# Split weight units of the input projection, stored to DRAM by the first token half and read back by the second

## The chip, the cores and the metric

One core of one Trainium2 chip runs the kernel. The metric is the device time of one execution in microseconds (us); lower is better. TensorE (PE) does the matmuls, VectorE (DVE), ScalarE (ACT) and GpSimd (POOL) work on arrays in on-chip memory, and SyncE (SP) issues the large transfers between DRAM and on-chip memory; they go out in the order of its one queue.

## The reference, cut to what matters

Two layers work on x (1024 tokens, 1024 wide). Each has a mixer and a channel part. The mixer begins with one input projection whose columns are divided among two groups of heads:

```python
proj = h @ w_in
g_q, g_k, g_v, g_o, g_a, m_q, m_kv, m_kpe = split_cols(proj, IN_SIZES)
...
o = gla_chunked(q, k, v, log_a)
o = rms_norm(o, gla_out_norm) * jax.nn.silu(g_o...)
...
mla_out = mla_attention(q_nope, q_pe, k_nope, k_pe, mv).reshape(B, S, D_MLA)
mixed = jnp.concatenate([gla_out, mla_out.astype(gla_out.dtype)], axis=-1)
return mixed @ w_out
```

The first group is a gated linear attention (q, k, v, output gate g, decay), the second a causal softmax attention with low-rank latents. Before the mixer and the channel part h is normed and modulated by a conditioning vector that comes from c @ w_ada ("ada"); the channel part is x + gate * (relu(h W1)^2 W2). Everything is float32.

## The kernel before

**Exactness.** A float32 product is made of three matmuls in a faster rounded format: both operands are split into a high part (the rounded value) and a low part (the rest), and `mm3` (L160 to L163) adds high x high, high x low and low x high. So every weight must be split in the kernel before TensorE can use it.

**Arena.** On-chip memory holds 51 slots of 128 x 1024 float32 (`Arena`, names s..., first in, first out: the slot that has been free longest is given out first). Weights pass through it in "units" of one slot each. `load` gets a slot and issues the transfer on SP's queue, `split` gets two more slots, casts the unit to its high part (L307; ScalarE, or VectorE where the unit's two letters begin with v) and subtracts it for the low part (L308; VectorE if the second letter is v, GpSimd if it is g). `get` prepares a unit and up to three after it (`LOOKAHEAD`), as long as slots are free; `drop` gives the two slots back.

**Units of the input projection.** For each layer and each half of the tokens (A: 0 to 511, B: 512 to 1023) there are 16: four L (latents and decay, 464 columns, two k-blocks each), four qk, four v and four g. Half A and half B use the same columns of w_in, and each loads and splits them for itself. In half A the v units are cast on VectorE and subtracted on GpSimd ("vg"), the others are "ag". In half B L and qk are "av", v and g "ag".

**Order.** The order in which the program is written comes from a list of steps, and the unit table follows it:

```python
"vA E X2 R LA Ha =1 TA QA X3 Hb WA gA OA LB TB QB X4 WB gB u00 P1 vB u01 a00 P1 "
```

vA, LA, QA and gA are the projections of half A and vB, LB, QB, gB those of half B (`inproj_tok` L595, and `queries_keys` for Q). WA and WB are the score matrices of the gated linear attention (`gla_scores` L896): a chain of seven levels, each with a decay on ScalarE (L955, L957), products on GpSimd (L927, L958) and VectorE (L956, L961), 128-column score matmuls on TensorE (L912) and a masked copy on VectorE (L966, L973); at its end are VectorE's L982, L988 and L990 and the transposes L998. X2, X3 and X4 load w_ada and make conditioning rows from it on VectorE (L254, L256). u00, u01 are head units of the softmax attention, a.. its blocks. xd is a buffer in DRAM to which x is moved while its slots are wanted otherwise (L1211; read back at L1235).

A list scheduler then puts the instructions of each engine in a fixed order from estimated times, so filling matmuls of a projection stand between those of a score chain. At most eight transfers of SP's queue are under way: each waits for one of eight completion semaphores, taken in turn.

## Time and profile before

| | us |
|---|---|
| median of the runs (3) | 2334.77 |
| lowest and highest | 2326.91, 2339.45 |
| profiled execution, its own time | 2329.49 |
| its span in the trace | 2327.7 |
| busy: TensorE | 2228.0 |
| busy: VectorE | 1785.4 |
| busy: ScalarE | 1137.8 |
| busy: GpSimd | 457.3 |

The span begins with the first instruction of the trace and ends with its last. Its mean granted clock of TensorE is 0.988 of full speed. Matmuls overlap in the records (a start every 0.21 to 0.23 us, a length of some 0.38 us), so "busy" counts a stretch without a gap as full; where TensorE waits, the busy time of a stretch is less than its length, and where the granted clock is under 1 the work in it took longer.

### The profile page before, as it was taken

What the parts mean: (1) busy time and instruction counts of PE and PEld (TensorE: products, weight loads), DVE (VectorE), ACT (ScalarE), POOL (GpSimd) and SP (SyncE); (2) the same over time, 40 slices, a digit from 0 to 9 for tenths busy, and PEclk for the clock granted to TensorE, in tenths of its full rate; (3) what the DMA queues carried; (4) which work ended last, traced back from release to release, by engine and by line L of the source; (5) the groups of instructions that cost most, each with busy time, mean ns of one, the idle gap of its engine ahead of it and who ended that gap; (6) DMA issues with size and microseconds to landing.
All of it is one profiled execution on the core that took longest, in us unless ns stands there. A gap on an engine that the chain in (4) does not pass through costs nothing.

```text
span 2327.7 us, 29242 instructions
## 1 busy us (share of the span) xinstructions
PE 2228.0 (96%) x11016; PEld 1851.0 (80%) x11016; DVE 1785.4 (77%) x2453; ACT 1137.8 (49%) x1764; POOL 457.3 (20%) x326
## 2 busy tenths in 40 slices
PE   7989999999999999998999999999999999999999
PEld 4778788888788877886888888887888888887887
DVE  5987769757989788889996756986665867887794
ACT  3464647535632483433535555665365228633341
POOL 2544533410030000000074345342002000000000
PEclk9999999999999999999999999999999999999999
DMA  9632210236678655765741221004354564365562
GB/s 345 202 105 81 82 30 1 82 106 221 207 220 276 192 163 200 243 229 193 241 138 34 63 61 41 10 10 125 130 160 138 184 196 145 113 231 195 166 208 82
DMA packets 236657, 340.41 MB, mean 146 GB/s; under 512 B 11078, under 2 KB 150500, under 8 KB 236516
## 3 DMA queue, kind: packets, MB, share of 16 engines
q1 hardware_dynamic: 235968, 338.08, 44.8%
q8 instruction: 86, 1.41, 0.3%
q14 instruction: 55, 0.45, 0.1%
q10 hardware_dynamic: 548, 0.48, 0.1%
HBM read 317.54 MB, written 20.97 MB: 145 GB/s over the span
## 4 chain that ended last, share of the span: by engine, by line
PE 66%; DVE 14%; DMA 7%; ACT 2%; issue 2%; POOL 1%; SPq 0%; DVEq 0%; ACTq 0%; POOLq 0%
PE ps_m L162 9%; PE ps_m L163 9%; PE ps_m L161 8%; PE ps_s L162 6%; PE ps_s L163 6%; PE ps_s L161 6%; PE ps_g L163 4%; PE ps_g L162 4%; PE ps_g L161 4%; DMA s<-in_w_mlp_down_dram 3%; PE ps_x L163 2%; PE ps_x L162 2%; DMA s<-in_w_ada_dram 2%; PE ps_x L161 2%; DMA s<-in_w_mlp_up_dram 2%
## 5 line engine op out<-in xcount | busy, mean ns | idle before, releaser
L307 ACT CAST s<-s 128x1024 fp32r<-128x1024 f32 (+2 forms) x306 | 314.8, 1035 | 474.1 <-DVE s L304 243.2
L162 PE MATMUL ps_m<-s,s 128*128 128x512 f32 (+2 forms) x1212 | 462.2, 382 | 15.4 <-DVE s L1273 15.4
L161 PE MATMUL ps_m<-s,s 128*128 128x512 f32 (+2 forms) x1212 | 460.4, 383 | 10.4 <-ACT s L1272 3.9
L163 PE MATMUL ps_m<-s,s 128*128 128x512 f32 (+2 forms) x1212 | 459.1, 379 | 1.6 <-DVE s L308 1.5
L308 POOL TENSOR_TENSOR s<-s,s 128x1024 fp32r<-128x1024 f32 (+2 forms) x90 | 229.2, 2558 | 1051.6 <-ACT s L307 696.5
L161 PE MATMUL ps_s<-s,s 128*128 128x512 f32 (+5 forms) x928 | 356.9, 388 | 9.0 <-ACT s L719 3.1
L163 PE MATMUL ps_s<-s,s 128*128 128x512 f32 (+5 forms) x928 | 354.6, 384 | 1.8 <-DVE s L308 1.3
L162 PE MATMUL ps_s<-s,s 128*128 128x512 f32 (+5 forms) x928 | 354.7, 383 | 0.0
L308 DVE TENSOR_TENSOR s<-s,s 128x1024 fp32r<-128x1024 f32 x224 | 270.0, 1217 | 55.8 <-ACT s L307 45.6
L304 DVE TENSOR_TENSOR s<-s,s 128x1024 f32<-128x1024 f32 x160 | 198.4, 1242 | 119.0 <-DMA s<-in_w_mlp_up_dram 81.7
L162 PEld LDWEIGHTS ps_m<-s,s 128*128 128x128 f32 x1212 | 230.4, 190 | 59.1 <-DVE s L1273 18.5
L161 PEld LDWEIGHTS ps_m<-s,s 128*128 128x128 f32 x1212 | 229.3, 189 | 54.9 <-ACT s L1272 6.1
L163 PEld LDWEIGHTS ps_m<-s,s 128*128 128x128 f32 x1212 | 230.0, 190 | 42.7 <-DVE s L308 2.5
L1272 ACT CAST s<-s 128x1024 fp32r<-128x1024 f32 x140 | 146.7, 1050 | 187.6 <-DVE s L1270 57.3
L161 PEld LDWEIGHTS ps_s<-s,s 128*128 128x128 f32 x928 | 174.7, 188 | 47.2 <-ACT s L719 6.1
L163 PEld LDWEIGHTS ps_s<-s,s 128*128 128x128 f32 x928 | 175.2, 189 | 37.8 <-issue 3.0
L162 PEld LDWEIGHTS ps_s<-s,s 128*128 128x128 f32 x928 | 175.4, 189 | 32.8 <-issue 1.5
L162 PE MATMUL ps_g<-s,s 128*128 128x512 f32 (+1 forms) x506 | 195.2, 387 | 0.7 <-DVE s L1273 0.7
L161 PE MATMUL ps_g<-s,s 128*128 128x512 f32 (+1 forms) x506 | 194.6, 388 | 0.0
L163 PE MATMUL ps_g<-s,s 128*128 128x512 f32 (+1 forms) x506 | 194.4, 387 | 0.1
L1273 DVE TENSOR_TENSOR s<-s,s 128x1024 fp32r<-128x1024 f32 x140 | 173.6, 1244 | 14.9 <-ACT s L1272 11.1
L162 PE MATMUL ps_x<-s,s 128*128 128x512 f32 (+3 forms) x362 | 124.2, 344 | 1.5 <-DVE s L743 1.5
(320 smaller groups left out, 3636.1 us busy)
## 6 DMA issues: line engine op xcount, KB each, us to landing
s<-in_w_mlp_up_dram SPq DMA_DIRECT2D x192, 512.0 KB, 4.8
s<-in_w_mlp_down_dram SPq DMA_DIRECT2D x192, 512.0 KB, 4.3
s<-in_w_ada_dram SPq DMA_DIRECT2D x80, 512.0 KB, 5.1
s<-in_w_in_dram SPq DMA_DIRECT2D x48, 512.0 KB, 3.8
s<-in_w_ada_dram SPq DMA_DIRECT2D x32, 256.0 KB, 4.1
xd<-s SPq DMA_DIRECT2D x16, 512.0 KB, 4.5
s<-in_w_out_dram SPq DMA_DIRECT2D x16, 512.0 KB, 4.3
s<-xd SPq DMA_DIRECT2D x16, 512.0 KB, 3.4
```

Source lines behind the costliest of these rows:

```text
L161: PE.matmul(o, lh, rh, start=start, stop=False)
L162: PE.matmul(o, lh, rl, start=False, stop=False)
L163: PE.matmul(o, ll, rh, start=False, stop=stop)
L304: V.tensor_tensor(raw[:, :n], raw[:, :n], u.second[:, :n], op=ALU.add if u.sign > 0 else ALU.subtract)
L307: (V.tensor_copy if u.eng[-2] == "v" else S.copy)(R(u.hi[:, :n]), raw[:, :n])
L308: (V if u.eng[-1] == "v" else G).tensor_tensor(R(u.lo[:, :n]), raw[:, :n], u.hi[:, :n], op=ALU.subtract)
L1272: S.copy(R(hi), t)
L1273: V.tensor_tensor(R(lo), t, hi, op=ALU.subtract)
```

## The change

After half A has used a unit, and before its slots are given back, `drop` writes its high and low part to a buffer in DRAM (two transfers on SP's queue). The unit of half B with the same columns has `first` set to that of half A: its `load` gets two slots and reads both parts back with two transfers, and its `split` does nothing. Half B no longer reads these columns of w_in. A store can go out as soon as the cast or subtraction that wrote its data is done. All lines after L282 stand up to 17 further down in the changed kernel: L292 of before is L297, L308 is L315, L912 is L929, L927 is L944, L958 is L975, L998 is L1015 and L1211 is L1228; L294 is the reload and L344 the store.

```diff
--- before.py
+++ after.py
@@ -282,12 +282,17 @@
 
     def add_unit(src, a, b, eng):
         u = Unit()
-        u.src, u.a, u.b, u.eng, u.more, u.other, u.sign = src, a, b, eng, None, None, 0
+        u.src, u.a, u.b, u.eng, u.more, u.other, u.sign, u.first, u.dram = src, a, b, eng, None, None, 0, None, None
         units.append(u)
         return u
 
     def load(u):
         n = u.a * u.b
+        if u.first is not None:
+            u.hi, u.lo = AR.alloc(), AR.alloc()
+            for i, a in enumerate((u.hi, u.lo)):
+                nc.sync.dma_start(a[:, :n], u.first.dram[i, :, 0:n])
+            return
         u.raw = AR.alloc()
         nc.sync.dma_start(u.raw[:, :n].rearrange("p (a b) -> p a b", a=u.a), u.src)
         if u.more is not None:
@@ -298,6 +303,8 @@
             nc.sync.dma_start(u.second[:, :n].rearrange("p (a b) -> p a b", a=u.a), u.other)
 
     def split(u):
+        if u.first is not None:
+            return
         n = u.a * u.b + (0 if u.more is None else u.more.shape[-1])
         raw = u.raw
         if u.other is not None:
@@ -331,6 +338,10 @@
             ustate["loaded"] += 1
 
     def drop(u):
+        if u.dram is not None:
+            n = u.a * u.b
+            for i, a in enumerate((u.hi, u.lo)):
+                nc.sync.dma_start(u.dram[i, :, 0:n], a[:, :n])
         AR.free(u.hi, u.lo)
 
     def uw(u, j, c0, n):
@@ -368,6 +379,12 @@
             elif kind == "D":
                 d = int(rest)
                 U[l, "wo", d] = add_unit(wo[:, :, d * P:(d + 1) * P], 8, P, "ag")
+
+        for kind in ("L", "qk", "v", "g"):
+            for q in range(4):
+                one, two = U[l, 0, kind, q], U[l, 1, kind, q]
+                one.dram = dp.tile([2, P, 1024], F32, tag=f"w{kind}{q}", name=f"w{kind}{q}")
+                two.first = one
         wu = w_mlp_up[l].rearrange("(k p) n -> p k n", p=P)
         wd = w_mlp_down[l].rearrange("(k p) n -> p k n", p=P)
         for stage, order, block in (
```

How it moves the instructions is seen on three engines. The first piece is SP's queue in layer 0, half A, from the load of unit qk0 (the first 128x8x128 row) to that of unit L3 (128x2x464). Before:

```order
L292 DMA s_106_741<-in_w_in_dram 128x8x128
L245 DMA s_95_634<-in_w_ada_dram 128x1024
L245 DMA s_96_637<-in_w_ada_dram 128x1024
L292 DMA s_109_771<-in_w_in_dram 128x8x128
L292 DMA s_103_711<-in_w_in_dram 128x2x464
L1211 DMA xd<-s_9_132 128x1024
```

and with the change (wL... is the DRAM buffer of an L unit):

```order
L297 DMA s_106_783<-in_w_in_dram 128x8x128
L245 DMA s_95_674<-in_w_ada_dram 128x1024
L344 DMA wL_121<-s_67_418 128x928
L245 DMA s_96_677<-in_w_ada_dram 128x1024
L344 DMA wL_122<-s_70_424 128x928
L297 DMA s_109_815<-in_w_in_dram 128x8x128
L344 DMA wL_123<-s_83_546 128x928
L297 DMA s_103_751<-in_w_in_dram 128x2x464
L344 DMA wL_123<-s_84_547 128x928
```

Stores of L units now stand between the loads of w_ada and w_in. From the first of the four loads of x (at 35.63 us in the timeline of before) up to L3 there were 15 transfers ahead of it and are now 28, of which 13 are stores. Up to the load of X3 with which VectorE begins there were 38 and are now 66.

The second piece is GpSimd in layer 0 during WB: L958 and L927 (L975 and L944 with the change) are the products of the scores, 128x1024 subtractions those of v units of half B, and 128x640 ones those of head units. Before:

```order
L308 TENSOR_TENSOR s_261_2463<-s_259_2460,s_260_2462 128x1024
L958 TENSOR_TENSOR s_228_2020<-s_204_1846,s_232_2027 128x128x4
L927 TENSOR_TENSOR s_232_2027<-s_203_1845,s_232_2027 128x512
L958 TENSOR_TENSOR s_229_2021<-s_204_1846,s_233_2028 128x64x8
L958 TENSOR_TENSOR s_228_2020<-s_204_1846,s_232_2027 128x32x16
L958 TENSOR_TENSOR s_229_2021<-s_204_1846,s_233_2028 128x16x32
L927 TENSOR_TENSOR s_233_2028<-s_203_1845,s_233_2028 128x512
L927 TENSOR_TENSOR s_232_2027<-s_203_1845,s_232_2027 128x512
L958 TENSOR_TENSOR s_228_2020<-s_204_1846,s_232_2027 128x8x64
L308 TENSOR_TENSOR s_275_2568<-s_273_2564,s_274_2567 128x640
L308 TENSOR_TENSOR s_247_2273<-s_245_2270,s_246_2272 128x1024
L308 TENSOR_TENSOR s_250_2303<-s_248_2300,s_249_2302 128x1024
```

With the change:

```order
L975 TENSOR_TENSOR s_218_2063<-s_197_1896,s_222_2070 128x256x2
L944 TENSOR_TENSOR s_222_2070<-s_196_1895,s_222_2070 128x512
L975 TENSOR_TENSOR s_217_2062<-s_197_1896,s_221_2069 128x128x4
L944 TENSOR_TENSOR s_221_2069<-s_196_1895,s_221_2069 128x512
L975 TENSOR_TENSOR s_218_2063<-s_197_1896,s_222_2070 128x64x8
L944 TENSOR_TENSOR s_222_2070<-s_196_1895,s_222_2070 128x512
L975 TENSOR_TENSOR s_217_2062<-s_197_1896,s_221_2069 128x32x16
L944 TENSOR_TENSOR s_221_2069<-s_196_1895,s_221_2069 128x512
L975 TENSOR_TENSOR s_218_2063<-s_197_1896,s_222_2070 128x16x32
L315 TENSOR_TENSOR s_253_2538<-s_251_2534,s_252_2537 128x640
L975 TENSOR_TENSOR s_217_2062<-s_197_1896,s_221_2069 128x8x64
```

The subtractions of v units are gone, one of a head unit stands ahead of the last product.

The third piece is TensorE at the end of WA in layer 0, where the first unit of LB begins (the four 128x464 matmuls L161; s47_171 before and s4_170 with the change is its high part). Before:

```order
L912 MATMUL ps_g_1297<-s19_159_1151,s47_156_1148 128x128 x4
L912 MATMUL ps_g_1303<-s19_159_1151,s47_156_1148 128x128 x4
L998 MATMUL ps_g_1319<-cs_81,s27_128_952 128x128 x4
L998 MATMUL ps_g_1325<-cs_81,s27_128_952 128x128 x4
L161 MATMUL ps_m_1625<-s47_171_1369,s0_115_835 128x464
L161 MATMUL ps_s_1626<-s47_171_1369,s0_115_835 128x464
L161 MATMUL ps_m_1627<-s47_171_1369,s0_115_835 128x464
L161 MATMUL ps_s_1628<-s47_171_1369,s0_115_835 128x464
L1042 MATMUL ps_g_1487<-s44_80_428,s11_154_1146 128x128 x4
L1048 MATMUL ps_g_1492<-s44_80_428,s33_164_1318 128x256 x2
L162 MATMUL ps_m_1625<-s24_172_1370,s0_115_835 128x464
```

With the change:

```order
L929 MATMUL ps_g_1239<-s19_159_1207,s47_156_1204 128x128 x4
L929 MATMUL ps_g_1253<-s18_158_1206,s24_157_1205 128x128 x4
L161 MATMUL ps_m_1683<-s4_170_1425,s0_115_883 128x464
L929 MATMUL ps_g_1259<-s18_158_1206,s24_157_1205 128x128 x4
L161 MATMUL ps_s_1684<-s4_170_1425,s0_115_883 128x464
L929 MATMUL ps_g_1273<-s19_159_1207,s47_156_1204 128x128 x4
L161 MATMUL ps_m_1685<-s4_170_1425,s0_115_883 128x464
L929 MATMUL ps_g_1279<-s19_159_1207,s47_156_1204 128x128 x4
L929 MATMUL ps_g_1293<-s18_158_1206,s24_157_1205 128x128 x4
L161 MATMUL ps_s_1686<-s4_170_1425,s0_115_883 128x464
L929 MATMUL ps_g_1299<-s18_158_1206,s24_157_1205 128x128 x4
L929 MATMUL ps_g_1313<-s19_159_1207,s47_156_1204 128x128 x4
```

The four matmuls that need only the high part stand between the score matmuls now. Ahead of the first score of WA stand 78 matmuls of gA, and 62 before. Elsewhere, in the attention blocks and the channel part, TensorE's order is the same in both kernels.

## Rows read from the trace of the kernel before

**Rows 1.** Page, parts 1 and 2: busy us; GB/s in 40 slices.
```profile
PE 2228.0 (96%) x11016; PEld 1851.0 (80%) x11016; DVE 1785.4 (77%) x2453; ACT 1137.8 (49%) x1764; POOL 457.3 (20%) x326
...
GB/s 345 202 105 81 82 30 1 82 106 221 207 220 276 192 163 200 243 229 193 241 138 34 63 61 41 10 10 125 130 160 138 184 196 145 113 231 195 166 208 82
```

**Rows 2.** Page, part 5: xcount | busy, mean ns | idle before.
```profile
L307 ACT CAST s<-s 128x1024 fp32r<-128x1024 f32 (+2 forms) x306 | 314.8, 1035 | 474.1 <-DVE s L304 243.2
...
L308 POOL TENSOR_TENSOR s<-s,s 128x1024 fp32r<-128x1024 f32 (+2 forms) x90 | 229.2, 2558 | 1051.6 <-ACT s L307 696.5
...
L308 DVE TENSOR_TENSOR s<-s,s 128x1024 fp32r<-128x1024 f32 x224 | 270.0, 1217 | 55.8 <-ACT s L307 45.6
```

**Rows 3.** Page, part 6: xcount, KB each, median us to landing.
```profile
xd<-s SPq DMA_DIRECT2D x16, 512.0 KB, 4.5
...
s<-xd SPq DMA_DIRECT2D x16, 512.0 KB, 3.4
```

**Rows 4.** Transfers, 36 to 62 us: total; issues, us to landing.
```profile
DMA packets 4607, 9.66 MB, mean 371 GB/s; under 512 B 320, under 2 KB 2476, under 8 KB 4604
...
s<-in_x_dram SPq DMA_DIRECT2D x3, 512.0 KB, 10.1
s<-in_w_in_dram SPq DMA_DIRECT2D x2, 512.0 KB, 6.9
```

**Rows 5.** Timeline of SP's queue: start us, length us, line, operation.
```profile
35.63 3.03 SPq L170 DMA_DIRECT2D s<-in_x_dram  x4
...
57.83 3.51 SPq L292 DMA_DIRECT2D s<-in_w_in_dram  x2
```

**Rows 6.** Timeline of TensorE: the first matmuls with unit L3, layer 0.
```profile
83.68 0.37 PE L161 MATMUL ps_s<-s,s 128*128 128x464 f32 x1
83.89 0.37 PE L162 MATMUL ps_s<-s,s 128*128 128x464 f32 x1
```

**Rows 7.** Stretches, WB: busy PE, PEld, DVE, ACT, POOL; PEclk, DMA share, GB/s.
```profile
260.00:280.00 20.00, 17.42 (x136) 15.63 (x134) 19.33 (x25) 18.99 (x36) 12.01 (x9) 1.00 0.18 47
280.00:300.00 20.00, 17.62 (x79) 14.54 (x80) 12.30 (x17) 5.92 (x12) 14.79 (x11) 0.91 0.10 30
```

**Rows 8.** Stretches, layer 1: the end of WA, then WB.
```profile
1300.00:1320.00 20.00, 15.53 (x102) 13.45 (x101) 19.67 (x29) 18.11 (x29) 3.52 (x2) 1.00 0.25 75
1400.00:1420.00 20.00, 15.57 (x118) 13.54 (x116) 19.19 (x24) 18.78 (x35) 12.47 (x8) 0.99 0.14 43
1420.00:1440.00 20.00, 19.82 (x87) 16.40 (x88) 10.51 (x17) 3.85 (x7) 13.08 (x11) 0.92 0.06 17
```

**Rows 9.** Timeline of GpSimd, layer 0, WB.
```profile
256.98 2.41 POOL L308 TENSOR_TENSOR s<-s,s 128x1024 fp32r<-128x1024 f32 x1 [1.38 <-DVE s L966]
...
279.15 11.20 POOL L308 TENSOR_TENSOR s<-s,s 128x640 fp32r<-128x640 f32 x5 [3.27 <-ACT s L307]
```

**Rows 10.** Timeline of VectorE, layer 0, WB; [idle before, releaser].
```profile
260.67 0.69 DVE L956 TENSOR_TENSOR s<-s 128x512 f32<-128x512 f32 x1 [2.80 <-POOL s L958]
...
278.23 1.21 DVE L982 TENSOR_TENSOR s<-s,s 128x1024 f32<-128x1024 f32 x1
279.36 2.55 DVE L990 TENSOR_TENSOR s<-s,s 128x1024 f32<-128x1024 f32 x1
```

**Rows 11.** Timeline of TensorE, layer 0, the end of WB.
```profile
282.06 1.10 PE L998 MATMUL ps_g<-cs,s 128*128 128x128 f32 x8 [2.17 <-DVE s L990]
```

**Rows 12.** Timelines of GpSimd and VectorE, layer 1, WB.
```profile
1393.68 2.40 POOL L308 TENSOR_TENSOR s<-s,s 128x1024 fp32r<-128x1024 f32 x1 [0.60 <-ACT s L307]
...
1416.07 2.55 DVE L990 TENSOR_TENSOR s<-s,s 128x1024 f32<-128x1024 f32 x1
```

**Rows 13.** Timelines of VectorE and TensorE, layer 0, WA.
```profile
129.08 0.75 DVE L254 TENSOR_SCALAR s<-s,cond 128x1024 f32<-128x1024 f32 x1 [4.31 <-DMA s<-in_w_ada_dram]
...
152.49 1.21 DVE L308 TENSOR_TENSOR s<-s,s 128x1024 fp32r<-128x1024 f32 x1
...
155.06 1.13 PE L912 MATMUL ps_g<-s,s 128*128 128x128 f32 x8 [1.29 <-DVE s L973]
```


## The prediction

> **What bounds the kernel now.** I read the first part of the page first: TensorE is busy for 2228.0 of 2327.7 us [rows 1]. Nothing that makes another engine cheaper can shorten the time except where TensorE waits for that engine, or runs at a lower granted clock because it has waited. So the second view was the table of stretches, and in it the columns of TensorE and of its clock. Of the stretches that this change touches, those with something to win are the score chain of token half B (program step WB, at 260 to 300 us in layer 0 and at 1400 to 1440 us in layer 1), and the score chain of half A (WA, at 137 to 174 us and around 1310 us). In [rows 7] TensorE is busy 17.42 and 17.62 of 20 us, and in the second stretch its mean granted clock is 0.91: 2.58 and 2.38 us idle, and 0.09 x 20 = 1.8 us of speed, 6.8 us in all. In layer 1, in the second and third row of [rows 8], it is 4.43, 0.18 and 0.01 x 20 + 0.08 x 20 = 1.8 us, 6.4 us in all. Everywhere else half B's projections run with TensorE full, so most of the work that the change removes is hidden already.
>
> The third view was the timeline of these stretches, to see who ends the waits, and the fourth the transfers at the start of layer 0, because the change's price is paid there: from 36 to 62 us the 16 DMA engines move 371 GB/s and are busy all the time [rows 4].
>
> **What is removed.** Per layer half B no longer splits its 16 units. That is 32 ScalarE casts of 1035 ns (33.1 us), 16 VectorE subtractions of 1217 ns (19.5 us; the L and qk units) and 16 GpSimd subtractions of 2558 ns (40.9 us; the v and g units) in the whole program [rows 2]. Against a bound on TensorE this is worth nothing as a sum; it counts where one of them stands in a chain that TensorE waits for. I found four such places.
>
> *WB, the start of the chain, both layers.* GpSimd subtracts a v unit at 256.98 for 2.41 us [rows 9], and the masked product L958 that belongs to the scores stands behind it on that engine; VectorE then waits 2.80 us for that product (first row of [rows 10]), and the whole chain of levels behind it is that much later. In layer 1 the same subtraction takes 2.40 us [rows 12]. In the new order of GpSimd no subtraction of a v unit is left among the score products, so I book -2.4 us for each layer.
>
> *WB, the end.* VectorE's last product L990 takes 2.55 us, and the one before it, L982, of the same shape and the same number of inputs, 1.21 (the last two rows of [rows 10]). The difference is that GpSimd began a run of five subtractions at 279.15 [rows 9]. TensorE waits 2.17 us for this L990 [rows 11]; in layer 1 it takes 2.55 us as well [rows 12]. Two of the run's five in layer 0 are head units, which remain, so I take 2.55 - 1.21 = 1.3 us in layer 0 and, with the remaining subtraction of a head unit likelier to fall there, 0.8 in layer 1. The lower clock follows the waits; if the waits are halved I take about 1 us of the 1.8 back in each. WB: -4.7 us in layer 0 and -4.2 in layer 1, out of 6.8 and 6.4. Both ends: 0, if the chain only waits for its next member (VectorE's own levels), and all 13.2 us.
>
> The Trainium skill states for the shared GpSimd and VectorE port (SBUF — State Buffer, section "SBUF: two separate sides") that it is an exclusive lock, and that a VectorE operation with two SBUF inputs is blocked for a whole GpSimd instruction. The trace agrees in kind: the two-input product took 2.55 us beside GpSimd and 1.21 alone. By that rule each GpSimd subtraction taken away could free VectorE for its whole length, which is the mechanism of the third rival below.
>
> *WA.* VectorE subtracts a unit of half B (L308, 1.21 us at 152.49) while TensorE waits for the level after it: the pair of scores at 155.06 waited 1.29 us for VectorE [rows 13]. In layer 1 TensorE is idle for 4.47 of the 20 us around that place (the first row of [rows 8]). The reloaded units have no such subtraction and no ScalarE cast (1.03 us) in the chain. Also four matmuls of the L projection, which need only the high half of a unit, now stand inside the score chain as filling (third piece of order). I take 2.0 us each: one subtraction, and most of a cast or of four matmuls (four times some 0.21 us). Ends: 0 and 4.5 (layer 1's idle time). Sum -4.0.
>
> **What is added.** Every unit of half A is stored twice, high and low (64 stores, 32.8 MB), and every unit of half B loads two arrays instead of one (64 reloads for 32 loads, 16.4 MB more). The direct price of such transfers is seen in the trace on arrays of the same 128x1024 shape: 4.5 us to land for a store to a buffer of the program's own in DRAM, 3.4 us for a read of it [rows 3]. No engine but SP's queue issues them, and the stores wait only for the cast and the subtraction that made their data, not for matmuls. So the question is the queue.
>
> *Layer 0, half A.* 13 stores stand ahead of the load of unit L3, which was the 16th transfer from the one at 35.63 us and is now the 29th (first piece of order). Ahead of it are now 28 transfers, 14.39 MB by their shapes. At 371 GB/s [rows 4] these take 38.8 us, so it is issued at about 74.4 us; before, it was the second of the pair at 57.83, which ends at 61.3 [rows 5]. While the engines were full, transfers took 6.9 to 10.1 us to land [rows 4]: it lands at 81 to 84.5. A cast (1.03) and a GpSimd subtraction (2.56) later [rows 2] both halves stand at 85 to 88 us. TensorE wants the first at 83.68 and the low half one matmul later [rows 6]. That is a stall of 1 to 4 us; I take 3.5, since the steps of the conditioning (X2), which sit in the same queue, are late by as much on VectorE.
>
> The same sum for the third conditioning load (X3), which let VectorE go on at 129.08 [rows 13]: 66 transfers of 34.06 MB are now ahead of it from 35.63, 91.8 us, so it is issued at 127.4 and lands at 132 to 137, 3 to 8 us late. Of that 3.5 are already paid by the stall above, and the new order puts 16 more matmuls of gA ahead of the first score: 16 x 0.21 = 3.4 us by the distance of the two starts in [rows 6], and a little more since gA's are 512 columns wide and not 464. So I book nothing more, and take 0.5 us off for waits of TensorE in half A that the later start covers. Net for half A of layer 0: +3.0 us. Ends: 0, when the queue keeps its place in the gaps after 62 us, and +12, when stores run at 3.4/4.5 of the loads' pace.
>
> *Layer 1, half A.* The bytes moved in the slices around 1165 to 1340 us are 138, 34 and 63 GB/s, the slices 21 to 23 of [rows 1]. 16.4 MB over about 150 us add 109 GB/s. That stays under 371, so I book 0; what hides it is the idle DMA time itself.
>
> *The reloads.* The low half of unit L0 of half B waits for a slot that the last scores of WA use, and then needs the 3.4 us of a read [rows 3], while TensorE has the closing matmuls of the scores and a few of gla_out (about 2.5 us) before it wants it. Formerly the subtraction's result came in about as late. I take +0.5 us for each layer; ends 0 and +3.4.
>
> **Sum.** -4.7 - 4.2 (WB) - 4.0 (WA) + 3.0 (half A of layer 0) + 1.0 (reloads) = -8.9 us. On the profiled run's own 2329.49 us that gives 2320.6. The median of the runs shown is 2334.77, 5.3 us above it, so the same sum there gives 2325.9. I predict **2325 us**.
>
> **The rivals.** A measurement of this kernel tells some 0.5%, 11.7 us, from no change; faster means below 2323.1, slower above 2346.4. The forecast lies close to the first bound.
>
> *Nothing is won.* The splits were hidden and the chains of WB and WA are VectorE's own level operations, which stay; then the gain is the 2 or 3 us at the end of WB, and half A's queue takes it back: 2332 to 2338. For it: TensorE is full in most of half B. Against it: the named waits on L990 and on L958.
>
> *The queue of layer 0 gets in the way.* With at most eight transfers under way, a store that is slow to land holds a place that a load needs. A store took 4.5 us where a read took 3.4 [rows 3]. If stores pass at 3.4/4.5 of the pace, the 28 ahead of X3 (14.3 MB, 38.6 us) take 51 us, 12.5 us more; X3 and unit g1 are then late by 16 to 20 us, of which the filling covers 3.6, and half A costs some 15 to 20 us. It decides from the point where the mean pace of loads and stores falls under about 310 GB/s. With the gains halved as the scores of half A start late, that is 2334.8 + 18 - 5 = 2348. The Trainium skill speaks for this one (DMA: Bandwidth & Descriptors, section "Anatomy of one DMA — SWDGE (gpsimd) path"): a transfer's fixed time is mostly the receipt of its last write, and heaviest where the target is HBM. The landing of 4.5 against 3.4 us agrees; what it does to the pace of a full queue no run here shows.
>
> *More is won.* VectorE is no longer blocked by GpSimd anywhere in the two chains: all of WB's 13.2 us but a remainder of 3 is won, and in WA 4.47 us less a remainder of 1.5 in each layer, -6; the queue finds its gaps and costs nothing. That is -16: 2318.6, or 2313.5 on the profiled run's base. The port rule above speaks for it, and against it that VectorE's own level operations are as many as before.
>
> **Chances.** Forecast 0.42, of which 0.25 lies under 2323.1, since its own range of 2317 to 2330 straddles the bound; nothing won 0.22; the queue 0.20, of which 0.01 stays within the bound; more won 0.16, of which 0.01 within. Faster 0.25 + 0.15 = 0.40; same 0.17 + 0.22 + 0.01 + 0.01 = 0.41; slower 0.19. The range from 2308 to 2344 leaves out most of the queue's case and a little on the side of more; it takes in -16 with the lower base, and the +12 of the queue against half of the gains.
>
> **What would show it.** Right: in WB the wait of 2.17 us before L998 (L1015 with the change) is gone or under 1 us, VectorE's wait for GpSimd's masked product is gone, and the granted clock after it stays near 1; TensorE stalls some 3 us at the first matmul of unit L3; the DMA share stays at 1 until after 100 us; ScalarE has 32 casts less. Wrong: a stall above 8 us in half A of layer 0, at L3, g1 or at the start of WA (the queue); the same idle 2.5 us in WB (nothing won); a new wait of the L or q projection of half B for a reload that waits for its slot.

## The result and the profile after

The changed kernel takes **2352.74 us** (median of 6 runs, 2349.20 to 2356.05) against 2333.31 for the kernel before in the same session (6 runs, 2326.91 to 2339.45): a ratio of 1.0084, 95% interval 1.0063 to 1.0104. It is slower by 19.4 us, outside the predicted range (2308 to 2344) and on the side with a chance of 0.19. The profiled execution took 2352.74 us, its span is 2351.0; rows below come from it.

The page's parts 1 and 2 after, for [rows 1]:

```profile
PE 2241.3 (95%) x11016; PEld 1863.2 (79%) x11016; DVE 1759.6 (75%) x2437; ACT 1109.8 (47%) x1732; POOL 415.2 (18%) x310
...
GB/s 353 306 267 138 137 45 10 28 135 196 194 183 259 260 170 162 242 212 209 253 224 238 137 122 68 19 1 99 138 174 121 186 200 149 102 247 188 167 209 81
```

VectorE, ScalarE and GpSimd are busy 25.8, 28.0 and 42.1 us less, and TensorE's matmuls are as many; its busy time is 13.3 us longer, which fits matmuls run at the lower clock (mean granted clock 0.977 against 0.988).

**Where the time goes.** One group of matmuls, the same 96 in both kernels, runs in each layer behind the score chain of half B (in layer 0 it begins some 77 us behind it). Its line, from the timeline grouped by source line (duration ns min/median/max, first and last start), for before and after:

```profile
L669 PE MATMUL ps_g<-cs,s x96: 271/273/330, 357.7 to 1568.4; 128*128 128x128 f32 x96
```

```profile
L686 PE MATMUL ps_g<-cs,s x96: 271/273/330, 382.5 to 1593.0; 128*128 128x128 f32 x96
```

Its first start is 24.8 us late and its last, in layer 1, 24.6: layer 0 loses all of it, and in layer 1 gains and losses cancel. I use this *marker* for every kernel below, as late by (layer 0, layer 1); the second number counts from the start, so it holds the first.

The table of stretches of after for the first half of the tokens, layer 0, and behind it that of before (columns as in [rows 7]):

```profile
60.00:80.00 20.00, 14.41 (x60) 12.14 (x59) 6.59 (x14) 6.32 (x13) 2.16 (x1) 0.83 1.04 385
80.00:100.00 20.00, 14.12 (x79) 12.52 (x77) 17.86 (x18) 6.15 (x8) 5.52 (x3) 0.91 0.97 363
100.00:120.00 20.00, 15.84 (x57) 12.76 (x58) 14.58 (x31) 7.86 (x11) 7.57 (x8) 0.66 0.37 127
...
140.00:160.00 20.00, 16.91 (x64) 13.04 (x63) 9.79 (x13) 7.40 (x12) 7.53 (x5) 0.83 0.96 355
```

```profile
60.00:80.00 20.00, 20.00 (x115) 17.94 (x114) 19.50 (x27) 6.87 (x10) 9.35 (x4) 1.00 0.86 302
80.00:100.00 20.00, 20.00 (x95) 16.05 (x94) 19.39 (x27) 10.20 (x14) 12.06 (x5) 1.00 0.55 165
100.00:120.00 20.00, 17.85 (x72) 13.40 (x71) 15.77 (x36) 11.71 (x20) 9.73 (x14) 0.91 0.36 121
```

From 60 to 120 us TensorE idles 15.6 us (20 minus its busy time, three rows) and loses 0.17, 0.09 and 0.34 of 20 us in clock, 12.0 us; before it was 2.2 and 1.8. That is 23.7 us more at most: a low clock costs nothing while TensorE waits, and from 94.12 to 103.58, inside the longest wait, the mean granted clock is 0.62, which takes 3.6 us out and leaves 20.1. In the last row of after a second pair of waits (0.48 and 2.61 us for the cast and subtraction of a g unit, at 147.77 and 151.58) and 0.17 x 20 us of clock add 6.5, and from 20 to 60 us after idles 1.6 us more and loses 2.4 more in clock. In all some 30 us: the first score matmul of WA starts at 169.33 where it started at 137.29, and 16 matmuls more stand ahead of it. With the 6.8 us that WB wins back (below) this comes out near the marker's 24.8.

Two waits make up the 15.6 us. Timelines of after, TensorE, ScalarE, VectorE and GpSimd in turn:

```profile
73.42 0.75 PE L161 MATMUL ps_s<-s,s 128*128 128x464 f32 x1 [5.59 <-ACT s L1026]
103.58 1.94 PE L263 MATMUL ps_x<-cs,s 128*128 128x128 f32 x8 [9.46 <-DVE s L256]
```

```profile
62.36 0.28 ACTq L537 DMA_DIRECT2D s<-in_positions_dram  x1
...
64.93 1.06 ACT L480 ACTIVATE s<-s 128x1024 f32<-128x1024 f32 x1 [8.17 <-DMA wv<-s]
...
69.84 1.06 ACT L480 ACTIVATE s<-s 128x1024 f32<-128x1024 f32 x1 [3.76 <-DMA s<-in_w_ada_dram]
```

```profile
72.06 0.17 DVE L408 TENSOR_SCALAR rs_v<-ssq 128x4 f32<-128x4 f32 x1 [14.39 <-ACT s L480]
...
89.67 4.21 DVE L449 SCALAR_TENSOR_TENSOR s<-tmp,mod,s 128x512 fp32r<-128x512 f32 x3
...
97.00 6.44 DVE L256 SCALAR_TENSOR_TENSOR s<-s,cond,s 128x1024 f32<-128x1024 f32 x2
```

```profile
96.90 5.45 POOL L315 TENSOR_TENSOR s<-s,s 128x1024 fp32r<-128x1024 f32 x2 [3.56 <-ACT s L314]
```

The *first wait*: ScalarE issues small loads itself (positions at L537, norm rows at L577 and L578, 4 KB and less) between its sums of squares (L480). The profile ends their delay with the landing of a v unit's store, then of a w_ada load. Everything behind them on ScalarE is late: L480, VectorE's L408 (14.39 us idle), the copies L1026 that TensorE needs. These loads held ScalarE in the kernel before as well, with loads alone under way, but there the positions went out at 43.63 and not at 62.36. ScalarE of before:

```profile
47.74 0.97 ACT L307 CAST s<-s 128x928 fp32r<-128x928 f32 x1 [8.06 <-DMA s<-in_positions_dram]
```

The *second*: TensorE wants X2's conditioning rows (L256, seven products), and the last two come after the norm steps L449, side by side with GpSimd's subtractions: 6.44 us for two that take 1.27 each alone, and three L449 in 4.21. In the kernel before all seven stand ahead of the norm steps on VectorE (L430 there):

```profile
74.51 1.63 DVE L256 SCALAR_TENSOR_TENSOR s<-s,cond,s 128x1024 f32<-128x1024 f32 x1
76.46 4.27 DVE L430 SCALAR_TENSOR_TENSOR tmp<-s,mod,s 128x512 f32<-128x512 f32 x4 [0.33 <-ACT s L480]
```

After, three stand ahead and four behind. This order is fixed before the kernel runs, and over all 17 kernels it goes with the wait: in the six with three or four products ahead (the changed kernel, e1, e5, e6, e7, e8) TensorE waits 6.4 to 9.5 us there, in the eleven with five or more at most 0.5.

On SP's queue X2's loads go out late. The w_ada loads, before and after:

```profile
41.05 12.29 SPq L245 DMA_DIRECT2D s<-in_w_ada_dram  x6
...
54.96 0.92 SPq L245 DMA_DIRECT2D s<-in_w_ada_dram  x2
```

```profile
70.89 0.33 SPq L245 DMA_DIRECT2D s<-in_w_ada_dram  x1
...
75.14 0.38 SPq L297 DMA_DIRECT2D s<-in_w_in_dram  x1
```

The last is issued at 70.89, where both of the last pair were out by 55.88. No wait of VectorE from 56 to 105 us ends with the landing of such a load, though: it waits 14.4 us for ScalarE and four times 1.1 to 1.3 for ScalarE and TensorE. The last row is unit L3: 75.14, predicted 74.4. The pace was no worse than in [rows 4] (transfers, 36 to 62 us, after):

```profile
DMA packets 3700, 10.54 MB, mean 405 GB/s; under 512 B 328, under 2 KB 1096, under 8 KB 3698
```

**WB and layer 1.** The stretches of after for [rows 7, 8], WB of layer 0 and then of layer 1:

```profile
280.00:300.00 20.00, 20.00 (x131) 18.09 (x130) 13.05 (x16) 13.49 (x24) 9.91 (x7) 1.00 0.34 111
300.00:320.00 20.00, 20.00 (x123) 17.69 (x122) 13.26 (x25) 10.36 (x23) 5.44 (x7) 1.00 0.09 28
...
1420.00:1440.00 20.00, 20.00 (x133) 18.12 (x132) 13.84 (x18) 15.35 (x27) 11.26 (x7) 1.00 0.28 98
1440.00:1460.00 20.00, 19.40 (x116) 16.75 (x116) 13.58 (x25) 9.83 (x21) 6.87 (x8) 1.00 0.11 33
```

TensorE waits for 0.6 us in them, in the last: the whole 6.8 us of the prediction's first part are won in layer 0, and all but 0.6 of its 6.4 in layer 1. But layer 1 pays them back in half A. TensorE, GpSimd and VectorE of after, layer 1:

```profile
1231.48 0.77 PE L161 MATMUL ps_m<-s,s 128*128 128x512 f32 x1 [7.13 <-DVE s L1415]
```

```profile
1216.88 1.18 POOL L594 TENSOR_TENSOR s<-cosT,grp 128x256 f32<-128x256 f32 x1
1218.03 2.33 POOL L596 TENSOR_TENSOR s<-sinT,grp 128x256 f32<-128x256 f32 x2
1220.32 7.75 POOL L315 TENSOR_TENSOR s<-s,s 128x928 fp32r<-128x928 f32 x3
```

```profile
1219.69 1.22 DVE L447 SCALAR_TENSOR_TENSOR tmp<-s,mod,tmp 128x512 f32<-128x512 f32 x1
...
1223.43 2.64 DVE L447 SCALAR_TENSOR_TENSOR tmp<-s,mod,tmp 128x512 f32<-128x512 f32 x1
```

Before, at the same place, GpSimd and then VectorE:

```profile
1191.71 6.26 POOL L308 TENSOR_TENSOR s<-s,s 128x928 fp32r<-128x928 f32 x1 [5.62 <-ACT s L307]
```

```profile
1194.52 0.74 DVE L430 SCALAR_TENSOR_TENSOR tmp<-s,mod,tmp 128x512 f32<-128x512 f32 x1
```

Before, one subtraction (128x928) stands ahead of GpSimd's rope products; it is drawn out to 6.26 us while VectorE does norm steps in 0.74 each. After, the products (L593 to L596) come first, and each VectorE step takes as long as one GpSimd instruction beside it: 1.22 by a product of 1.18, 2.64 by a subtraction of 7.75/3 = 2.58. So L1415 is late, and TensorE waits 7.13 us and runs at 0.83 from 1220 to 1240.

### The profile page after: what moved, and what is told of

The parts are those of the page before. It is cut to its first block, busy times and chain, and to the rows that moved or that the text cites. A ratio compares the mean times of both kernels' runs of the same rounds, so it can differ in the third digit from the quotient of the medians.

```text
span 2351.0 us, 29364 instructions
## 1 busy us (share of the span) xinstructions
PE 2241.3 (95%) x11016; PEld 1863.2 (79%) x11016; DVE 1759.6 (75%) x2437; ACT 1109.8 (47%) x1732; POOL 415.2 (18%) x310
## 4 chain that ended last, share of the span: by engine, by line
PE 71%; DVE 14%; DMA 9%; ACT 3%; issue 2%; POOL 1%; SPq 0%; DVEq 0%; ACTq 0%; POOLq 0%
PE ps_m L162 9%; PE ps_m L163 9%; PE ps_m L161 9%; PE ps_s L162 7%; PE ps_s L163 7%; PE ps_s L161 7%; PE ps_g L163 4%; PE ps_g L161 4%; PE ps_g L162 4%; DMA s<-in_w_mlp_down_dram 3%; DMA s<-in_w_ada_dram 2%; PE ps_g L929 2%; PE ps_x L162 2%; PE ps_x L163 2%; PE ps_x L161 2%
## 5 line engine op out<-in xcount | busy, mean ns | idle before, releaser
L314 ACT CAST s<-s 128x1024 fp32r<-128x1024 f32 (+2 forms) x274 | 282.4, 1037 | 431.0 <-DVE s L311 263.9
L161 PE MATMUL ps_m<-s,s 128*128 128x512 f32 (+2 forms) x1212 | 462.9, 385 | 18.2 <-DVE s L1415 7.1
L161 PE MATMUL ps_s<-s,s 128*128 128x512 f32 (+5 forms) x928 | 362.4, 394 | 9.8 <-ACT s L1026 5.6
L315 POOL TENSOR_TENSOR s<-s,s 128x1024 fp32r<-128x1024 f32 (+2 forms) x74 | 183.6, 2491 | 1044.2 <-ACT s L314 707.2
L163 PE MATMUL ps_s<-s,s 128*128 128x512 f32 (+5 forms) x928 | 358.2, 387 | 4.5 <-DVE s L449 3.2
L162 PE MATMUL ps_s<-s,s 128*128 128x512 f32 (+5 forms) x928 | 359.6, 388 | 0.0
L315 DVE TENSOR_TENSOR s<-s,s 128x1024 fp32r<-128x1024 f32 x208 | 251.6, 1220 | 55.0 <-ACT s L314 47.1
L161 PEld LDWEIGHTS ps_m<-s,s 128*128 128x128 f32 x1212 | 230.6, 191 | 63.3 <-issue 8.0
L163 PEld LDWEIGHTS ps_m<-s,s 128*128 128x128 f32 x1212 | 231.2, 191 | 42.1 <-DVE s L315 1.3
L161 PEld LDWEIGHTS ps_s<-s,s 128*128 128x128 f32 x928 | 177.4, 191 | 48.5 <-ACT s L736 6.1
L163 PEld LDWEIGHTS ps_s<-s,s 128*128 128x128 f32 x928 | 178.0, 192 | 39.1 <-DVE s L449 3.4
L162 PEld LDWEIGHTS ps_s<-s,s 128*128 128x128 f32 x928 | 177.9, 192 | 33.2 <-issue 1.5
L161 PE MATMUL ps_g<-s,s 128*128 128x512 f32 (+1 forms) x506 | 194.6, 388 | 0.8 <-DVE s L1336 0.8
L1290 DVE TENSOR_TENSOR s<-s,s 128x1024 fp32r<-128x1024 f32 x140 | 173.5, 1244 | 14.8 <-ACT s L1289 11.0
```

Source lines behind the costliest of these rows:

```text
L161: PE.matmul(o, lh, rh, start=start, stop=False)
L162: PE.matmul(o, lh, rl, start=False, stop=False)
L163: PE.matmul(o, ll, rh, start=False, stop=stop)
L314: (V.tensor_copy if u.eng[-2] == "v" else S.copy)(R(u.hi[:, :n]), raw[:, :n])
L315: (V if u.eng[-1] == "v" else G).tensor_tensor(R(u.lo[:, :n]), raw[:, :n], u.hi[:, :n], op=ALU.subtract)
L1290: V.tensor_tensor(R(lo), t, hi, op=ALU.subtract)
```

## The experiments

Times are medians; "marker" is lateness in layer 0 and layer 1 of the profiled execution. Two profiles whose layer 0 is that of before (e4, e15) have +2.1 there, so 2 us of it mean nothing, and a profiled execution can lie 5 or 6 us off its kernel's median (e5: 2369.49 against 2364.34; e11: 2326.26 against 2332.28).

**e1, e2: the small loads off ScalarE's queue**, in the changed kernel and in the one before.

```diff
-nc.scalar.dma_start(posi, ...)   # and the norm rows
+nc.gpsimd.dma_start(posi, ...)
```

> The changed kernel; the five small loads of layer 0 (positions and four rows of norm weights) go out from GpSimd's queue instead of ScalarE's, all else as in the changed kernel. Theory S (ScalarE's queue): in the changed kernel ScalarE stands still from 56.8 to 64.9 and from 66.1 to 69.8 us because its small loads wait for a completion semaphore that a store holds, VectorE waits 14.39 us for ScalarE's L480, and TensorE loses about 8 us at 73 us and a good part of the 9.46 us at 94 to 104 us; without it the time falls by 10 to 18 us, to 2335 to 2343. Rival Q (the bytes in the one queue): the loads themselves are late by the stores ahead of them, ScalarE's wait only stands in front of a wait that comes anyway; the time stays within 4 us of 2352.7.

> The kernel before with the same edit, as a control. ScalarE stands 8.06 us there too, at 39.7 to 47.7 us, and TensorE loses 2.6 us at 51.9 us. Theory S: 0 to -4 us against the kernel before. Rival Q: 0.

e1: 2344.27, ratio 1.0041 (1.0025 to 1.0057), marker +12.1, +13.6. The first wait is gone and 8.5 us of 19.4 come back (10 by the two ratios); the second stays (9.32 us at 94.82), though VectorE's 14.39 us fell to 2.2. e2: 2343.24, ratio 1.0033 (1.0017 to 1.0050), marker +12.3, +18.0, where I expected a small gain: a wait of TensorE in half A for ScalarE's L431 grows from 2.6 to 5.1 us, and one of 4.6 us for conditioning rows (L267) appears in WA. So e1 isn't a pure removal: the same edit costs 9 us where no store is in the way, and 8.5 us may understate what the first wait costs. Five small loads moved are worth 9 us here; a difference of that size between two kernels can come from their order alone.

**e3, e8: fewer stores.** e3 stores one pair (v0) and every unit of half B reads it; e8 stores and reads the high part alone.

```diff
-one.dram = dp.tile(...); two.first = one
+two.first = U[l, 0, "v", 0]      # e3: only that unit has a dram
```

> The changed kernel with only unit v0 of half A stored in each layer; every unit of half B reads that one pair back (two loads of the same size as in the changed kernel), so half B computes with the wrong columns. 60 of the 64 stores are gone, all 64 reloads stay, no split in half B. If the stores are the price (theories S and Q alike): all of the 28 us of layer 0 half A and most of the 8.5 us of layer 1 come back, and the gains in the score chains of half B stay (about 8.5 and 6.5 us): 2315 to 2322. Rival R (the reloads, their slots and the moved order are the price): 2340 or more.

> The changed kernel with the high part alone stored (32 of the 64 stores), and half B reading that part for both, so half B computes with wrong low parts. Reloads and missing splits as in the changed kernel. If the price goes with the number of stores: half of some 31 us comes back, 2335 to 2339. If the queue has a threshold in layer 0 (loads late only when the engines are full for longer than the slack of 8 to 14 us): nearly all comes back, 2322 to 2330.

e3: 2322.53, ratio 0.9941 (0.9918 to 0.9964), marker +2.4, -4.5: reloads without stores win 12 us (2334.18 before, same session). It has one new wait, for a reload in front of LB:

```profile
185.55 0.47 PE L162 MATMUL ps_m<-s,s 128*128 128x464 f32 x1 [3.64 <-DMA s<-wv]
```

e8: 2338.74, ratio 1.0032 (1.0017 to 1.0046), marker +15.3, +9.1: half the stores, 0.0032 left of the 0.0084; but against e3, which has the gains without the price, that is 0.0091 of 0.0143, more than half. Layer 1 wins 6.2 us (9.1 against 15.3), since its half A has no wait for L1415.

**e7, e6: the stores alone, and the stores on GpSimd's queue.**

```diff
-two.first = one                                     # e7
-nc.sync.dma_start(u.dram[i, :, 0:n], a[:, :n])      # e6
+nc.gpsimd.dma_start(u.dram[i, :, 0:n], a[:, :n])
```

> The changed kernel with its 64 stores, but half B loads and splits its own units as in the kernel before and reads nothing back. The price without the gain: by the traces some 23 us more in half A of layer 0 and 8.5 in layer 1, no gain in the score chains of half B: 2358 to 2368. If the moved order and the slots of the reloads have a share in half A's loss, less than 2352.

> The changed kernel with all 64 stores issued by GpSimd's queue instead of SP's. The same bytes move; SP's order and its eight completion semaphores are free of them, but each store costs GpSimd some 0.5 to 0.7 us (its issue of a small load in the first experiment) and a wait for its data. Theory L (the price is the place in SP's queue and the semaphores): the stall of ScalarE at 57 to 70 us and most of half A's loss go, 2325 to 2338, less what GpSimd's 64 issues cost. Rival B (the price is the bytes on the 16 DMA engines): 2345 or more.

e7: 2370.62, ratio 1.0165 (1.0143 to 1.0186), marker +34.8, +42.9: the price without the gain, 39 us over the before of that session (2331.38). e6: 2357.40, ratio 1.0110 (1.0092 to 1.0129), marker +23.2, +25.9: another queue doesn't help as a whole. The first wait is gone, but ScalarE waits 11.4 and 10.9 us for loads of w_in between 40 and 80 us, and GpSimd now spends its own time on issuing (0.57 us for one at 1203.32), so the price of SP's queue isn't measured alone.

**e4, e5, e9 to e12: parts of the change.** Layer 1 alone, and some kinds of units in both layers.

```diff
-for kind in ("L", "qk", "v", "g"):
+for kind in ("L", "qk", "v", "g") if l == 1 else ():   # e4
+for kind in ("v",):                                    # e5; e9 L, qk, g; e10 qk, g; e11 qk; e12 g
```

> The change in layer 1 alone; layer 0 loads and splits as before. In the changed kernel layer 1 lost 8.5 us in half A and won 5 to 6.5 us in half B: 2333 to 2337 by the two traces, the kernel before being 2333. If the loss of layer 1 was a chance meeting of GpSimd's subtractions with VectorE's norm steps that the new slot order of layer 0 brought, it is gone and the time is 2326 to 2328.

> The change for the four v units of each layer alone; L, qk and g are loaded and split by both halves as before. 16 of the 64 stores stay (8 in each layer, in layer 0 the first that go out, at 37 to 62 us). Theory P (each store in the full queue costs what it delays): in layer 0 eight stores of 1.3 to 1.4 us put the loads behind them back by 11 us, of which TensorE sees 0 to 8; layer 1 loses 0 to 2; the gains in the score chains of half B, which came from the v units' subtractions on GpSimd, stay at 4 to 8 us each: 2321 to 2332. Rival (the loss is one threshold, passed as soon as the queue is full): half A of layer 0 still loses 20 us or more, 2342 or more.

> The change for L, qk and g units; v units are loaded and split by both halves as before. Theory F (the loss in half A comes from the stores that go out while the queue is full, and in layer 1 from the v stores that put the first L unit behind the rope products in GpSimd's order): layer 1's loss of 8 to 9 us is gone, layer 0 keeps part of it for the L stores at 50 to 75 us (5 to 12 us). Theory O (half B's gain comes from TensorE's order: 12 and not 54 matmuls between the first two pairs of scores, the rest spread to the end): the gain in the score chain stays, 8 and 5 us, although the subtractions of v units are back. 2324 to 2334. Rival V (the gain comes from the v subtractions on GpSimd, as predicted): no gain there, 2337 or more.

> The change for qk and g units alone: 32 stores, which go out from about 75 us on, behind the loads of L3 and the conditioning (X2). Theory F with O: half A of layer 0 loses 0 to 5 us, layer 1 nothing, the score chains of half B win 8 and 5 us: 2316 to 2325, under the kernel before. Rival V: 2331 or more.

> The change for qk units alone: 16 stores from about 90 us on. TensorE's order between the pairs of scores has the spread form here as well (16, 12, 19, 19, 19, 22 matmuls). Theory O: the score chains win 4 to 8 us each, half A loses 0 to 3: 2317 to 2327. Rival V: 2331 or more.

> The change for g units alone: 16 stores at 100 us and later, where the queue has room. TensorE's order keeps 56 matmuls between the first two pairs of scores in layer 0. Theory O: no or little gain in the score chain of half B, none lost in half A: 2327 to 2334. Rival V gives the same; a rival by which every GpSimd subtraction in half B counts (8 fewer of 2.5 us): 2325 or less.

| units | us | ratio (95%) | marker |
|---|---|---|---|
| e4, all, layer 1 | 2334.77 | 1.0006 (0.9991 to 1.0020) | +2.1, +3.0 |
| e5, v | 2364.34 | 1.0145 (1.0114 to 1.0175) | +24.5, +39.4 |
| e9, L, qk, g | 2331.23 | 0.9998 (0.9984 to 1.0013) | -0.1, +1.7 |
| e10, qk, g | 2332.37 | 1.0001 (0.9986 to 1.0017) | +4.5, +4.3 |
| e11, qk | 2332.28 | 0.9996 (0.9983 to 1.0009) | 0.0, -2.7 |
| e12, g | 2339.15 | 1.0025 (1.0012 to 1.0039) | +5.5, +15.3 |

e5 missed its expectation by over 30 us, and that was the turn: the v units, whose subtractions I had blamed in WB, win nothing there and cost 33 us by themselves; layer 0 still loses 24.5, as the rival in its expectation had it. The stretches of e5 in WB, then those of e9, in which the v units are split again:

```profile
280.00:300.00 20.00, 17.22 (x126) 15.80 (x124) 14.89 (x19) 15.23 (x27) 11.63 (x9) 1.00 0.26 80
300.00:320.00 20.00, 17.96 (x97) 15.61 (x98) 13.14 (x23) 9.02 (x19) 6.22 (x7) 0.91 0.17 54
```

```profile
260.00:280.00 20.00, 20.00 (x132) 18.12 (x131) 15.39 (x18) 16.29 (x29) 8.33 (x7) 1.00 0.16 43
280.00:300.00 20.00, 19.66 (x111) 16.66 (x110) 16.33 (x22) 9.92 (x20) 12.22 (x10) 1.00 0.20 53
```

e5 idles 4.8 us and loses 1.8 of clock, as before; e9 has a v unit's subtraction on GpSimd in the middle of WB (257.72, 2.38 us) and is full. What they differ in is TensorE's order: the starts of the score pairs (L912, L929) lie evenly 6.1 us apart in e9 (251.18, 257.28, 263.39, 269.50), as in after:

```profile
280.65 1.95 PE L929 MATMUL ps_g<-s,s 128*128 128x128 f32 x16
286.75 1.95 PE L929 MATMUL ps_g<-s,s 128*128 128x128 f32 x16
292.86 1.95 PE L929 MATMUL ps_g<-s,s 128*128 128x128 f32 x16
```

In the kernel before they crowd at the end, with waits:

```profile
264.45 2.22 PE L912 MATMUL ps_g<-s,s 128*128 128x128 f32 x16 [0.28 <-DVE s L973]
267.35 2.02 PE L912 MATMUL ps_g<-s,s 128*128 128x128 f32 x16 [0.68 <-DVE s L973]
```

e5's crowd too (289.61, 294.47). So the gain of WB in layer 0 goes with filling matmuls that are spread over the chain, not with the subtractions. Over all kernels, by TensorE's idle time from 2 us ahead of the first score to 6 us behind the last: the seven in which 60 or more matmuls stand between two score pairs idle 3.8 to 5.3 us; of the ten that have at most 22 in a place, nine idle 0.3 or less, but e11 idles 3.9. Spread matmuls alone don't do it, then, and in layer 1 e9 has them too and still loses 3.7 of the 6.4 us of before (18.12 us busy at a clock of 0.91 from 1400 to 1420).

e9 wins WB of layer 0 and is no faster: by the same measure it idles 12.4 us in the scores of half A, where before idles 9.1. e10 missed by 7 us: TensorE idles 15.5 us in the same scores (5.1 for VectorE's L990 and 4.0 for ScalarE's L972). e11 missed by 5 us, with 12.1 us there. e12 missed by 5; why it loses 10 us in layer 1, with no long wait for L1415 (0.9), stays open.

**e13, e14, e15: bytes or places.** e13 has all 64 stores, 62 of them 64 columns wide; e14 was to write each layer's stores behind its last load of half A, and e15 to do so in layer 1 and leave layer 0 as before. Their edit does less: it holds the stores of the v units alone, until the first unit of another kind is dropped, and puts an order edge from each store to the weight load written last by then.

```diff
-one.dram = dp.tile([2, P, 1024], ...)               # e13; all units of half B read v0's pair
+one.dram = dp.tile([2, P, 64], ...)
-nc.sync.dma_start(u.dram[i, :, 0:n], a[:, :n])      # e14; e15 with layer 1 alone
+held.append(u)    # v units: stored when a unit of another kind is dropped, with an order edge to the last load so far
```

> All 64 stores stand in SP's queue where the change has them, but 62 of the 64 carry 64 columns instead of 1024 (the pair of unit v0 is stored whole, and all units of half B read that pair back, so half B's projection has wrong weights). Bytes: the stores cost by what they move, then this runs like the kernel in which only one pair was stored, 2320 to 2328. Places: the stores cost by the place that each holds in the queue and among the transfers under way until its receipt, and by the order that they give to GpSimd, then most of the loss stays, 2340 to 2352, with ScalarE again held at L480 and TensorE waiting over 6 us for L1415 in layer 1.

> The changed kernel with every store of a layer's half A emitted behind the last weight load of that half, in one run; GpSimd's order at the start of layer 1 is again that of the kernel before. Order: the loss of half A came from loads that stood behind stores, and in layer 1 from GpSimd's order; then no wait over 3 us for L1415 in layer 1 and at most 5 us lost by 115 us in layer 0, and with the gain of 15 us in WB the time is 2320 to 2332. Bytes: 33 MB more have to pass while the half runs, and only another place pays: 2340 to 2352, with the wait moved to the third conditioning load.

> The change in layer 1 alone, with that layer's stores emitted behind its last weight load of half A. Order: the kernel with the change in layer 1 alone took 2334.8 and lost some 8 us at the start of its half A to the wait for L1415; without that wait 2324 to 2330, faster than the kernel before by 4 to 9 us. Bytes: the wait or its like stays, 2332 to 2338.

e13: 2332.79, ratio 0.9999 (0.9988 to 1.0009), marker +5.4, -1.2: in between its two cases. Against the changed kernel 0.0085 of the time (20 us) go with the bytes, and against e3 0.0058 (14 us) stay. The smaller stores also gave VectorE another order (six of the seven L256 ahead of the norm steps) and put GpSimd's subtraction ahead again in layer 1, so the 20 us are those of bytes and orders together. In layer 0 the second wait is gone and TensorE's three largest waits between 60 and 140 us are 4.4, 0.9 and 0.8; ScalarE still holds VectorE for 7.48 us (14.39 after). e14: 2339.72, ratio 1.0027 (1.0015 to 1.0038), marker +11.4, +8.4: above its case of order (2320 to 2332), just under that of bytes (2340 to 2352). Its eight v stores go out at 80.27 to 87.88 us instead of 37 to 60, and loads of w_in still stand behind stores (issued at 91.49, 99.41, 121.32 and 127.32). So it doesn't test what its expectation says, stores behind all loads; it shows that with the v stores held back both waits of layer 0 are gone and 11 us are still lost. The waits moved: 2.21 us for the subtraction of a unit loaded late (90.34), 4.75 for ScalarE (102.20), 3.05 for another late unit (141.32). e15: **2327.81**, ratio 0.9978 (0.9964 to 0.9991), marker +2.1, -5.0: faster than the kernel before by 5 us and than e4 by 0.0028 of the time, some 6.5 us. The interval is clear of 1, but the gain is inside the 0.5% by which the prediction called two kernels the same. Its v stores go out at 1197.33 to 1203.33, where those of e4 began at 1170.12. GpSimd, VectorE and TensorE of e15, where after has its wait of 7.13:

```profile
1192.82 6.26 POOL L315 TENSOR_TENSOR s<-s,s 128x928 fp32r<-128x928 f32 x1 [5.62 <-ACT s L314]
```

```profile
1195.62 0.74 DVE L457 SCALAR_TENSOR_TENSOR tmp<-s,mod,tmp 128x512 f32<-128x512 f32 x1
```

```profile
1203.04 0.47 PE L161 MATMUL ps_m<-s,s 128*128 128x512 f32 x1 [1.66 <-DVE s L1425]
```

Over all kernels the split is complete: in the six with the rope products ahead of that subtraction (the changed kernel, e1, e4, e5, e6, e7) TensorE waits there 7.1 to 8.0 us, in the other eleven at most 2.3.

## Why the prediction was wrong

**Layer 0, half A, "+3.0 us" with ends 0 and +12: this is the step that failed.** It measured about 30 (20.1, 6.5 and 4.0 above). The load of L3 was reckoned rightly: 75.14 (74.4 predicted), and no stall there at all. X3's loads at 123.76 to 129.21 (127.4) are luck: my sum took 371 GB/s to the end, and from 100 to 120 us 127 moved. The sign that I had named, a stall above 8 us in half A, came at another matmul. What I left out is who else stood in those queues and what order the other engines would get. I priced X2, which sits among the same stores, at L3's 3.5 us; its last load went out 15 us late, its products were put behind the norm steps on VectorE, and TensorE waited 9.5 for them. "No engine but SP's queue issues them" was true of the stores, but not of what waits beside them: ScalarE's own small loads waited for a store to land, and its in-order work with them (5.6 us on TensorE; e1). And I priced waits as idle time alone, where 15.6 us of idle cost some 8 of clock on top (12.0 less the 3.6 that fell into a wait). e3, e8 and e13 show that it is the stores, and mostly their bytes with the orders that the scheduler makes of them: with few or tiny stores the marker of layer 0 falls from +24.8 to +2.4 and +5.4, with half of them to +15.3. The second wait goes with VectorE's order in all kernels, and GpSimd's collisions are 5.9 us in its rows (4.21 - 3 x 0.74 and 6.44 - 2 x 1.27); but no kernel changes that order alone, so whether late loads would have made TensorE wait in the old order stays open.

**Layer 1, half A, "0": wrong by about 8 us.** Bytes had room there, as I said (e15 moves as many and waits 1.66 us), but the stores also changed the order that the scheduler gave to GpSimd. The price fits the port rule of the Trainium skill (SBUF — State Buffer, section "SBUF: two separate sides": whichever of the two starts first holds the shared port for its whole instruction): VectorE's steps grew to the length of GpSimd's. The rule gives no sum by itself; in the other order GpSimd was drawn out, to 6.26 us, and TensorE waited 0.85 us before and 1.66 in e15. That order goes with the wait in all 17 kernels, but e15 changes the order of the v stores and of GpSimd together; no kernel here changed GpSimd's alone.

**WB, "-4.7 and -4.2": sizes too small, cause wrong.** 6.8 and 5.8 us were won. My cause, v subtractions on GpSimd, fell with e5 (gone, nothing won) and e9 (there, all won but 0.3 us in these rows). What fits best is TensorE's order, which no kernel changes alone and which e11 and layer 1 of e9 show not to be enough. Why the scheduler spreads it in some kernels stays open.

**WA, "-2.0 each": not won in layer 0, and 0.8 us in layer 1** (idle 4.5 before, 3.6 after, with no clock lost in either). TensorE's waits in layer 0 by their ends, 130 to 190 us after, and 100 to 190 before (us in total, times, longest):

```profile
PE ps_m L162 <- POOL s L315: 2.6, 1, 2.6
PE ps_m L161 <- DVE s L1041: 1.9, 1, 1.9
PE ps_g L929 <- DVE s L955: 1.2, 1, 1.2
```

```profile
PE ps_g L912 <- DVE s L973: 5.0, 6, 1.3
PE ps_g L912 <- DVE s L966: 3.7, 1, 3.7
```

TensorE's waits for VectorE in the scores shrink from 8.7 us to 2.3, but a late g unit (2.6), the wait for L1041 (1.9) and, beyond these rows, one of 2.25 for ScalarE (199.01) take their place.

**Reloads, "+0.5 each, ends 0 and +3.4": right.** TensorE waits 0.5 us for one in layer 0 and 1.2 in layer 1; the upper end was met by e3's 3.64.

**The rivals.** The queue's case had nearly the time (2348) and the right place, but not its mechanism: it was to decide where the pace fell under 310 GB/s, and the pace rose to 405. Its sentence that a store "holds a place that a load needs" fits ScalarE's loads, whose delay the profile ends with a store's landing. The case of more won had the right size for WB: without stores (e3) the gain is 12 of the 16 us that it forecast.

## What to carry to other kernels

Before adding transfers to a queue, list every load behind them with its consumer, on the other engines' queues too, and price each delay where its consumer stands; a queue at full pace is not a queue without a price. A wait of TensorE in a full stretch cost its idle time and, here, up to half as much (7.13 and 3.4 us) or as much (3.1 and 3.4 us) again in clock. Where a scheduler fixes the order, a change that adds or removes transfers also changes the order of every engine: compare those orders first, of the bounded engine and of its helpers, since here the second wait of layer 0, the wait of layer 1 and the gain of WB in layer 0 went with them. And try to hold back what nobody waits for: with the v stores of layer 1 alone held back, the time is the lowest of the kernels that compute the right result (2327.81), 5 us under the kernel before.

## What was not expected of the hardware

Loads and stores together moved more bytes per time than loads alone: 405 against 371 GB/s over the same 26 us; the packets under 2 KB were 1096 against 2476, so direction and packet size are not told apart. Loads of 4 KB and less on ScalarE's queue held that engine up while large transfers of SP's queue were under way: 8.17 and 3.76 us idle with stores among them, 8.06 with loads alone. VectorE's norm step with two inputs in on-chip memory took 0.74 us, 1.22 or 2.64 by what GpSimd did beside it, and GpSimd's subtraction (128x928) 2.58 or 6.26 by the order of the two.
